# First norm of a decoder layer: loads, transposes, scaling and splitting in a new order

## The chip, the cores and the metric

The kernel runs on one core of a Trainium2 chip. The metric is device time in microseconds for one execution of the whole program; of the kernel before it is 2183.67 us, the median of three runs (2179.38 to 2184.96). The engines are named as in the profile: PE (TensorE), PEld (its weight load), DVE (VectorE), ACT (ScalarE), POOL (GpSimd), SP (SyncE, which issues most DMA transfers).

## The reference

One layer of a hybrid decoder for a prompt of 1024 tokens and 8 sequences of one new token each, D_MODEL 1024, all in float32. What the change touches is the very start, the conditioned norm `h = rmsnorm(x, w) * (1 + scale1) + shift1`:

```python
def _adaln(c, w_mod, b_mod):
    m = jax.nn.silu(c) @ w_mod + b_mod
    return jnp.split(m[:, None, :], 6, axis=-1)

sh1, sc1, gt1, sh2, sc2, gt2 = _adaln(c, lp['w_mod'], lp['b_mod'])
h = _rmsnorm(x, lp['norm1_w']) * (1 + sc1) + sh1
qkv, gdn_gate, beta_raw, a_raw, sq, sk, sv, ga, gb = _split_in(h @ lp['w_in'])
```

From `h @ w_in` come the operands of a gated delta rule (8 heads), of a sliding-window attention with sinks (16 query heads, 4 key heads), and two branch gates. Then follow the output projection, a second conditioned norm, a gated FFN of width 2816 with a causal convolution, and a last norm. Besides the two outputs y, ten states are returned.

## The kernel before

All activations stand transposed, columns of D_MODEL on the partitions: eight tiles of 128, called k = 0 to 7. The 1032 tokens (1024 and 8) are cut into three parts of 384, 384 and 264 (`PARTS`). A product in float32 is made of three in the `fp32r` format: each operand is split into a high part, rounded, and a low part, the rest, and `mm3` (lines 177 to 182) adds hi*hi, hi*lo and lo*hi. So `b1h` and `b1l`, one pair for each part, are the split h, and `wh` and `wl` a split weight of 1024 x 128.

The first norm has these pieces, all within `run`:

- `conditioning` makes silu(c), transposed, in `cT`; `vectors` loads small vectors and turns them.
- `modulation(lo)` loads a chunk of w_mod of 1024 x 512 in four transfers of 512 KB (tag `qst`, eight slots), multiplies (line 264, four products a transfer pair, 32 x 512), copies the result (line 267), turns it with `strips` (line 270) and adds the bias (line 271). Chunks 8 and 12 give scale1 of columns k = 0 to 3 and 4 to 7, chunks 0 and 4 give shift1 of the same. `norm_scale` (line 274) makes `a1` = (1 + scale1) * w.
- `norm_part` loads the tokens of a part as rows in up to three tiles (tags `raw` or `qst`), takes the sums of squares on ACT (line 291), the power -1/2 on POOL (line 125), puts the factors on diagonals, and multiplies these with ones (line 299), so that `r` holds each token's factor on all partitions (copied at line 301).
- `turn_part` turns the tiles on PE (line 190) and copies them on DVE (line 318) into four "rooms" for a part (three for the third), slots that later stages use for other things (`ROOMS`; the tags are V, kh, kl, obt, wmh, wml, raw, qst). It stores the turned x to DRAM (`xT`, line 331) for the residual.
- `modulate` does for one k: multiply the tile by a1 and r (line 341, DVE), add the shift and round (line 342, ACT), and take the rest (line 343, DVE).

In `run` the chunks go in the order 8, 0, 12, 4; the first part is loaded and turned after chunk 8, the second after chunk 12, the third after chunk 4. The first part is modulated as soon as its shifts are there, the second and third at the beginning of `attention`. Then come the first keys and queries: `project` with `w[0]` (keys) and `w[1]` (queries), part by part, each 24 products a part, into PSUM tiles `mm` of a pool with two slots. `k_out` and `q_out` copy and split the result (lines 537 to 540 and 562 to 563). Behind them come the queries of the second pair, values, and the attention groups with late modulation chunks, decays and states in between.

The order of instructions on each engine isn't written by hand here: a scheduler of the framework sorts the program by its own model of times when the kernel is built, and the engines then run these orders strictly, waiting on semaphores. `issue_after(ins)` lets an instruction stand in that order only behind `ins`.

Of the kernel before, what the change touches and what calls it, by code (L numbers as in the profile page):

```python
# [64 lines left out]
class Step:  # L65
# [118 lines left out]
    def new_parts(self):  # L184
        return [(self.t(self.b1, [P, KC, n], f"b1h{t}", F32R), self.t(self.b1, [P, KC, n], f"b1l{t}", F32R))
                for t, (_, n) in enumerate(PARTS)]

    def transpose(self, out, in_):
        p = in_.shape[0]
        self.nc.tensor.transpose(out, in_, self.ident[:p, :p])  # L190


    def vectors(self, pool, psum):
# [4 lines left out]
        nc.sync.dma_start(rows[0:48, 0, :], I["b_mod"][0].rearrange("(n p) -> n p", p=P))  # L198
        nc.sync.dma_start(rows[48:56, 0, :], I["norm1_w"][0].rearrange("(n p) -> n p", p=P))
        nc.sync.dma_start(rows[56:64, 0, :], I["norm2_w"][0].rearrange("(n p) -> n p", p=P))  # L200
        nc.sync.dma_start(rows[64:65, 0, :], I["gdn_onorm_w"])
        nc.sync.dma_start(rows[0:96, 1, :], I["gdn_conv_w"][0].rearrange("j (n p) -> (j n) p", p=P))
        rows2 = self.t(pool, [P, P], "pp")
        nc.sync.dma_start(rows2[0:66, :], I["ffn_conv_w"][0].rearrange("j (n p) -> (j n) p", p=P))
        nc.sync.dma_start(rows2[66:88, :], I["ffn_conv_b"][0].rearrange("(n p) -> n p", p=P))
# [14 lines left out]
    def conditioning(self, pool, psum):  # L220

        nc, I = self.nc, self.I
        c = self.t(pool, [9, NP], "qst", bufs=8)
        nc.sync.dma_start(c[0:8, :], I["c_sample"])
        nc.sync.dma_start(c[8:9, :], I["c_prompt"])
        th = self.t(pool, [9, NP], "qst", bufs=8)
        nc.scalar.activation(th, c, AF.Tanh, scale=0.5)
        s2 = self.t(pool, [9, NP], "qst", bufs=8)
# [22 lines left out]
    def modulation(self, pool, psum, ptag, lo, tags, rtag):  # L251
# [4 lines left out]
        for k0 in range(0, KC, 4):  # L256
# [6 lines left out]
            for j in range(4):  # L263
                nc.tensor.matmul(ps[32 * j:32 * j + 32], self.cT[:, k0 + j, :], ws[j // 2][:, j % 2, :],
                                 start=k0 == 0, stop=k0 > 0)
        rows = self.t(pool, [P, 512], rtag)
# [11 lines left out]
    def norm_part(self, pool, psum, t, tags):  # L278
# [19 lines left out]
        ps = self.t(psum, [P, 512], "pv")[:, :n]  # L298
# [5 lines left out]
    def turn_part(self, pool, psum, t, xs, tags):  # L304
# [6 lines left out]
        for c, x in enumerate(xs[:n // P]):  # L311
            k = 0
            for room in rooms:
                m = room.shape[1]
                ps = self.t(psum, [P, 4, P], "pv" if room is rooms[-1] else "pt")[:, :m]
                for i in range(m):
                    self.transpose(ps[:, i, :], x[:, (k + i) * P:(k + i + 1) * P])
                nc.vector.tensor_copy(room[:, :, c * P:(c + 1) * P], ps)
                k += m
# [9 lines left out]
        for room in rooms:  # L329
            m = room.shape[1]  # L330
            nc.sync.dma_start(self.xT[k:k + m, :, c0:c0 + n].rearrange("k p n -> p k n"), room)
# [3 lines left out]
    def modulate(self, pool, t, k, raw, r, a, sh):  # L335

        nc = self.nc
        n = PARTS[t][1] // P * P
        hi, lo = (x[:, k, :n] for x in self.h[t])
        v, s = self.t(pool, [P, 512], ("pc", "E")[k % 2])[:, :n], self.mT[:, sh + k, 8:9]  # L340
        nc.vector.scalar_tensor_tensor(v, raw, a[:, k, 8:9], r[:, :n], op0=ALU.mult, op1=ALU.mult)
        nc.scalar.activation(hi, v, AF.Identity, bias=s)
        nc.vector.scalar_tensor_tensor(lo, v, s, hi.bitcast(F32), op0=ALU.add, op1=ALU.subtract)
# [103 lines left out]
    def attention(self, pool, psum):  # L447
# [13 lines left out]
        w, raws, rs = self.start  # L461
        for t in (1, 2):
            if len(raws[t]) > KC:
                self.modulate_samples(pool, t, raws[t][KC], rs[t], self.a1, 0)
            for k in range(KC):
                self.modulate(pool, t, k, raws[t][k], rs[t], self.a1, 0)
# [1329 lines left out]
    def run(self):  # L1796
        S, nc = ExitStack, self.nc
        self.constants()
        with S() as ca:
            with S() as c:  # L1800
# [5 lines left out]
                self.h = self.new_parts()  # L1806
                self.xT = self.t(self.dr, [KC, P, NT], "xT")
                self.a1 = self.const([P, KC, 9], "a1")
                rs, raws = {}, {}
# [91 lines left out]
```

## Time and profile before

| | |
|---|---|
| median of 3 runs | 2183.67 us (2179.38 to 2184.96) |
| profiled execution, its own time | 2182.87 us |
| its span | 2181.1 us |
| PE busy | 2101.2 us, 96% |
| DVE busy | 1344.9 us, 62% |
| ACT busy | 789.0 us, 36% |
| POOL busy | 311.5 us, 14% |
| granted TensorE clock, mean | 0.972 |
| moved by DMA | 223.91 MB, mean 103 GB/s |

Times in a timeline are microseconds from the span's start. A row of a timeline has start, duration, engine, line, operation, tiles (output, then inputs), shape and count; at the end in brackets the idle time of the engine ahead of it and what released it. [...] In the groups by line, "xcount | busy, mean ns | idle before" follow the shapes.

### The profile page before, as it was taken

How to read it: one execution, taken by the hardware profiler on the slowest of the kernel's cores; microseconds unless marked ns; L12 is line 12 of the kernel's file. 1: busy time of each engine (PE TensorE's matmuls, PEld its weight loads, DVE VectorE, ACT ScalarE, POOL GpSimd, SP SyncE). 2: the span in 40 equal slices, each digit the busy share in tenths (PEclk: the TensorE clock that was granted, in tenths of full speed). 3: DMA queues.
4: the chain of work that ended last, by engine and by line, in shares of the span. 5: the costliest groups of instructions: out<-in, count | busy, mean ns of one | idle time of the engine just before them, and what ended most of it. 6: DMA issues, size and time to landing. Idle time of an engine off the chain costs nothing.

```text
span 2181.1 us, 41178 instructions
## 1 busy us (share of the span) xinstructions
PE 2101.2 (96%) x16514; PEld 1982.5 (91%) x16514; DVE 1344.9 (62%) x2907; ACT 789.0 (36%) x2010; POOL 311.5 (14%) x422
## 2 busy tenths in 40 slices
PE   7899999999899999999999999999999999999998
PEld 3886777899898998999999999999999999999998
DVE  5756676375655756765324665478876867866565
ACT  3445456333234344334322032344433433421102
POOL 1000000020321210111111200002232233100000
PEclk9999999999999989999999999999999999999999
DMA  9333323151232221221318844523222232263202
GB/s 345 113 108 114 117 74 97 48 147 47 71 84 60 71 68 40 63 65 50 91 60 237 250 152 126 155 67 98 79 88 69 78 98 68 97 224 121 85 3 79
DMA packets 265114, 223.91 MB, mean 103 GB/s; under 512 B 57586, under 2 KB 232469, under 8 KB 264906
## 3 DMA queue, kind: packets, MB, share of 16 engines
q1 hardware_dynamic: 263354, 216.83, 32.7%
q10 hardware_dynamic: 1152, 3.70, 0.4%
q8 instruction: 130, 2.13, 0.4%
q0 software_dynamic: 416, 0.75, 0.1%
q14 instruction: 62, 0.51, 0.1%
HBM read 171.25 MB, written 52.33 MB: 103 GB/s over the span
## 4 chain that ended last, share of the span: by engine, by line
PE 61%; DVE 4%; DMA 4%; ACT 2%; issue 1%; SPq 1%; POOL 1%; POOLq 0%; DVEq 0%; ACTq 0%
PE mm L180 14%; PE mm L182 13%; PE mm L181 13%; PE wv L181 3%; PE wv L180 3%; PE wv L182 3%; PE wy L182 2%; PE wy L180 2%; PE wy L181 2%; PE tp L190 1%; DMA b1l<-dlr 1%; PE rc L909 1%; PE rc L905 1%; PE rc L902 1%; DMA b2l<-ob 1%
## 5 line engine op out<-in xcount | busy, mean ns | idle before, releaser
L180 PE MATMUL mm<-b1h,wh 128*128 128x384 f32 (+1 forms) x1440 | 474.3, 331 | 8.2 <-DVE kl L540 4.3
L182 PE MATMUL mm<-b1h,wl 128*128 128x384 f32 (+1 forms) x1440 | 467.4, 326 | 0.6 <-DVE wl L130 0.5
L181 PE MATMUL mm<-b1l,wh 128*128 128x384 f32 (+1 forms) x1440 | 467.3, 325 | 0.0
L180 PEld LDWEIGHTS mm<-b1h,wh 128*128 128x128 f32 x1440 | 273.4, 190 | 17.4 <-issue 3.1
L182 PEld LDWEIGHTS mm<-b1h,wl 128*128 128x128 f32 x1440 | 272.7, 190 | 6.9 <-issue 4.4
L181 PEld LDWEIGHTS mm<-b1l,wh 128*128 128x128 f32 x1440 | 273.9, 190 | 4.5 <-issue 4.0
L130 DVE TENSOR_TENSOR wl<-raw,wh 128x1024 fp32r<-128x1024 f32 x76 | 93.5, 1230 | 81.1 <-ACT wh L129 80.2
L129 ACT ACTIVATE wh<-raw 128x1024 fp32r<-128x1024 f32 x77 | 80.6, 1047 | 168.3 <-PE mm L181 96.6
L180 PE MATMUL mm<-b2h,wh 128*128 128x384 f32 (+1 forms) x384 | 124.4, 324 | 1.8 <-ACT wh L129 1.7
L180 PE MATMUL mm<-pk,w 128*128 128x260 f32 (+1 forms) x440 | 124.7, 283 | 1.0 <-ACT pk L129 0.6
L181 PE MATMUL mm<-pk,w 128*128 128x260 f32 (+1 forms) x440 | 124.4, 283 | 0.8 <-DVE pk L130 0.8
L182 PE MATMUL mm<-b2h,wl 128*128 128x384 f32 (+1 forms) x384 | 122.9, 322 | 1.8 <-DVE wl L130 1.8
L182 PE MATMUL mm<-pk,w 128*128 128x260 f32 (+1 forms) x440 | 124.4, 283 | 0.0
L181 PE MATMUL mm<-b2l,wh 128*128 128x384 f32 (+1 forms) x384 | 123.2, 321 | 0.0
L182 PE MATMUL mm<-bmh,pk 128*128 128x256 f32 (+1 forms) x380 | 109.0, 287 | 0.9 <-DVE pk L130 0.7
L180 PE MATMUL mm<-bmh,pk 128*128 128x260 f32 (+1 forms) x380 | 108.7, 286 | 0.2 <-ACT pk L129 0.2
L1382 DVE SCALAR_TENSOR_TENSOR x<-mm,mT,x 128x256 f32<-128x256 f32 (+2 forms) x133 | 63.5, 480 | 70.6 <-PE mm L182 70.3
L181 PE MATMUL mm<-bml,pk 128*128 128x260 f32 (+1 forms) x353 | 100.8, 285 | 0.0
L180 PE MATMUL mm<-bmh,w 128*128 128x260 f32 (+1 forms) x320 | 90.9, 284 | 0.0
L182 PE MATMUL mm<-bmh,w 128*128 128x260 f32 (+1 forms) x320 | 90.8, 284 | 0.0
L130 DVE TENSOR_TENSOR w<-ws,w 128x512 fp32r<-128x512 f32 x88 | 60.2, 685 | 41.8 <-ACT w L129 41.7
L180 PEld LDWEIGHTS mm<-pk,w 128*128 128x128 f32 x440 | 82.9, 188 | 1.6 <-ACT pk L129 0.8
(595 smaller groups left out, 5701.0 us busy)
## 6 DMA issues: line engine op xcount, KB each, us to landing
raw<-in_w_in_dram SPq DMA_DIRECT2D x60, 512.0 KB
bml<-act SPq DMA_DIRECT2D x22, 516.0 KB
raw<-in_w_ffn_gate_dram SPq DMA_DIRECT2D x22, 512.0 KB
raw<-in_w_ffn_up_dram SPq DMA_DIRECT2D x22, 512.0 KB
raw<-in_w_ffn_down_dram SPq DMA_DIRECT2D x22, 512.0 KB
qst<-in_w_mod_dram SPq DMA_DIRECT2D x16, 512.0 KB
raw<-in_w_mod_dram SPq DMA_DIRECT2D x16, 512.0 KB
act<-fa SPq DMA_DIRECT2D x22, 260.0 KB
```

What stands on the lines that cost most here:

```text
L129: self.nc.scalar.activation(hi, x, AF.Copy)
L130: (eng or self.nc.vector).tensor_tensor(lo, x, hi.bitcast(F32), op=ALU.subtract)
L180: mm(ps, whi, xhi, start=first, stop=False, **kw)
L181: mm(ps, whi, xlo, start=False, stop=False, **kw)
L182: mm(ps, wlo, xhi, start=False, stop=last, **kw)
L190: self.nc.tensor.transpose(out, in_, self.ident[:p, :p])
L902: yield step(nc.tensor.matmul(ks, K[:, n, :], S, start=True, stop=True))
L905: yield step(nc.tensor.matmul(sp, W[:, n, :], y, start=True, stop=True))
L909: yield step(nc.tensor.matmul(ds, kd[:, n, :], s, start=True, stop=True))
L1382: nc.vector.scalar_tensor_tensor(x[:, :np_], ps[:, :np_], self.mT[:, m + j, 8:9], x[:, :np_], op0=ALU.mult, op1=ALU.add)
```

## The change

The loads, the turning and the splitting of the first norm get another order, and some of the work other engines.

- The chunks still go 8, 0, 12, 4, but the second part is loaded and turned after chunk 0, and the third behind chunk 4.
- Behind chunk 0 the columns 0 to 3 of the first two parts are scaled, shifted and split. Behind chunk 12 their columns 4 to 7 are scaled only; the scaled tiles stand unsplit in `vs`, which is the room of the third part's `b1h` and `b1l`, until chunk 4 gives their shifts (`shift_tile`). The third part's operands take that room behind it.
- All stores to xT wait, in SP's order, until the third part's x is issued (`store_turned`).
- Odd columns of the second and third part are scaled on ACT and multiplied by r on POOL (`scale_tile`); three of four rooms of the second part, and two of three of the third, are copied by ACT instead of DVE.
- The small loads of `vectors` are issued by ACT; `conditioning` uses the slots kh and kl.
- The projections of the first keys and queries go keys of parts one and two, queries of parts one and two, keys of part three, queries of part three, with a third PSUM slot; the keys of the first two parts stand behind the second part's last turns and the last product of chunk 4.

```diff
     def vectors(self, pool, psum):
-        nc.sync.dma_start(rows[0:48, 0, :], I["b_mod"][0].rearrange("(n p) -> n p", p=P))
+        nc.scalar.dma_start(rows[0:48, 0, :], I["b_mod"][0].rearrange("(n p) -> n p", p=P))
...
     def modulation(self, pool, psum, ptag, lo, tags, rtag):
...
+        self.chunks.append(at.ins)
...
     def turn_part(self, pool, psum, t, xs, tags):
...
+                if t == 1 and c == 2:
+                    self.turned.append(turned.ins)
+                if t and room is not rooms[0]:
+                    nc.scalar.copy(room[:, :, c * P:(c + 1) * P], ps)
+                else:
+                    nc.vector.tensor_copy(room[:, :, c * P:(c + 1) * P], ps)
...
-            nc.sync.dma_start(self.xT[k:k + m, :, c0:c0 + n].rearrange("k p n -> p k n"), room)
+            self.stores.append((self.xT[k:k + m, :, c0:c0 + n].rearrange("k p n -> p k n"), room))
...
+    def store_turned(self):
+        for dst, room in self.stores:
+            with self.tc.issue_after(self.x_load.ins):
+                stored = self.nc.sync.dma_start(dst, room)
+        self.x_load = stored
+
+    def scale_tile(self, v, t, k, raw, r):
+        nc = self.nc
+        r, a = r[:, :v.shape[1]], self.a1[:, k, 8:9]
+        if t and k % 2:
+            nc.scalar.activation(v, raw, AF.Copy, scale=a)
+            nc.gpsimd.tensor_tensor(v, v, r, op=ALU.mult)
+        else:
+            nc.vector.scalar_tensor_tensor(v, raw, a, r, op0=ALU.mult, op1=ALU.mult)
+
+    def shift_tile(self, v, t, k):
+        hi, lo = (x[:, k, :v.shape[1]] for x in self.h[t])
+        s = self.mT[:, k, 8:9]
+        self.nc.scalar.activation(hi, v, AF.Identity, bias=s)
+        self.nc.vector.scalar_tensor_tensor(lo, v, s, hi.bitcast(F32), op0=ALU.add, op1=ALU.subtract)
...
     def attention(self, pool, psum):
...
-        for t in range(3):
-            self.project(w[0], h, k_out, (t,))
-            self.project(w[1], h, q_out, (t,))
+        self.mm = [self.pmm, self.pmm, self.pmf]
+        for ts in ((0, 1), (2,)):
+            for t in ts:
+                with ExitStack() as c:
+                    for ins in self.turned + self.chunks[(3, 3)[t]:(3, 3)[t] + 1] if t < 2 else ():
+                        c.enter_context(self.tc.issue_after(ins))
+                    self.project(w[0], h, k_out, (t,))
+            self.project(w[1], h, q_out, ts)
+        self.mm = [self.pmm]
...
     def run(self):
...
+                vs = [self.t(self.b1, [P, 4, 384], f"b1{x}2") for x in "hl"]
...
                 for lo in (8, 0, 12, 4):
                     self.modulation(pool, psum, "sc", lo, (("qst", 8),), "mrows")
+                    if lo in (8, 12):
+                        self.norm_scale(self.a1, 8, self.n1w, lo - 8, lo - 4)
+                    if lo in (8, 0):
+                        part(lo == 0)
+                        w.append(self.win((COL_SQ, COL_SK)[lo == 8]))
+                    if lo == 0:
+                        for t in range(2):
+                            self.modulate(pool, t, range(4), raws[t], rs[t])
+                    for t in range(2) if lo in (12, 4) else ():
+                        for k in range(4, KC):
+                            v = vs[t][:, k - 4, :]
+                            if lo == 12:
+                                self.scale_tile(v, t, k, raws[t][k], rs[t])
+                            else:
+                                self.shift_tile(v, t, k)
+                self.h.append(self.new_part(2))
+                part(2)
+                self.store_turned()
+                self.modulate_samples(pool, 2, raws[2][KC], rs[2], self.a1, 0)
+                self.modulate(pool, 2, range(KC), raws[2], rs[2])
```

Since a scheduler sets the orders, three places show what moved. The line numbers are those of each kernel (line 264 before is line 263 of the change, 190 is 189, 331 is 344). The first is SP's queue around the last modulation chunks, before:

```order
L288 DMA qst_338<-in_x_prompt_dram 128x1024
L288 DMA qst_346<-in_x_prompt_dram 128x1024
L288 DMA qst_354<-in_x_prompt_dram 128x1024
L331 DMA xT_154<-V_210 128x4x384
L261 DMA qst_424<-in_w_mod_dram 128x2x512
L331 DMA xT_154<-kh_211 128x2x384
L331 DMA xT_154<-kl_212 128x2x384
L261 DMA qst_426<-in_w_mod_dram 128x2x512
L261 DMA qst_432<-in_w_mod_dram 128x2x512
L261 DMA qst_434<-in_w_mod_dram 128x2x512
```

and in the changed kernel (`raw_838` is the weight of the next query pair):

```order
L260 DMA qst_445<-in_w_mod_dram 128x2x512
L260 DMA qst_447<-in_w_mod_dram 128x2x512
L135 DMA raw_838<-in_w_in_dram 128x8x128
L260 DMA qst_453<-in_w_mod_dram 128x2x512
L260 DMA qst_455<-in_w_mod_dram 128x2x512
L288 DMA qst_488<-in_x_prompt_dram 128x1024
L288 DMA qst_496<-in_x_prompt_dram 128x1024
L288 DMA qst_504<-in_x_sample_dram 8x1024
L344 DMA xT_154<-V_211 128x4x384
L344 DMA xT_154<-kh_212 128x2x384
L344 DMA xT_154<-kl_213 128x2x384
```

The stores of the first part have moved from ahead of the last chunk's quarters (424 to 434 before, 445 to 455 now) to behind the third part's x. The second place is PE at the last chunk of the changed kernel. `qst_296` and `qst_304` are the second and third x tile of the second part, and `qst_455` takes the slot of `qst_304`; `mm_648` are the first keys of the first part:

```order
L270 MATMUL sc_427<-strips_119,mrows_425 128x9 x4
L189 MATMUL pt_352<-ident,qst_304 128x128 x2
L263 MATMUL sc_444<-qst_445,cTr_116 32x512 x2
L263 MATMUL sc_444<-qst_447,cTr_116 32x512 x2
L189 MATMUL pt_356<-ident,qst_304 128x128 x2
L263 MATMUL sc_444<-qst_453,cTr_116 32x512 x2
L189 MATMUL pt_360<-ident,qst_304 128x128 x2
L263 MATMUL sc_444<-qst_455,cTr_116 32x512 x2
L180 MATMUL mm_648<-b1h_10_148,wh_258 128x384
L181 MATMUL mm_648<-b1l_11_149,wh_258 128x384
L182 MATMUL mm_648<-b1h_10_148,wl_259 128x384
```

Before, PE had the keys of the first part (`mm_646`), and behind them its queries, between the products of its third chunk (`sc_312`), a whole chunk earlier:

```order
L270 MATMUL sc_290<-strips_119,mrows_288 128x9 x4
L264 MATMUL sc_312<-qst_313,cTr_116 32x512 x2
L264 MATMUL sc_312<-qst_315,cTr_116 32x512 x2
L264 MATMUL sc_312<-qst_321,cTr_116 32x512 x2
L180 MATMUL mm_646<-b1h_10_148,wh_260 128x384
L181 MATMUL mm_646<-b1l_11_149,wh_260 128x384
L182 MATMUL mm_646<-b1h_10_148,wl_261 128x384
```

So no product of keys or queries runs ahead of the last chunk any more, and the turns of the second part stand between its quarters. The third place is ACT behind the last chunk. There the changed kernel has (line 361 is the shift and rounding, 321 a copy of a room, 301 the copy of r; lines 564, 565 and 589 split keys and queries, 537, 538 and 562 before):

```order
L321 COPY qst_519<-pv_530 128x2x128
L361 ACTIVATE b1h_10_148<-b1h_14_152,mT 128x384 x4
L361 ACTIVATE b1h_12_150<-b1l_15_153,mT 128x384 x4
L321 COPY raw_518<-pt_525 128x3x128
L321 COPY qst_519<-pv_544 128x2x128
L301 COPY pp_515<-sc_513 128x264
L564 ACTIVATE kh_642<-mm_648 64x384
L565 ACTIVATE kh_642<-mm_648 64x384
L589 ACTIVATE qst_646<-mm_714 64x384
L564 ACTIVATE kh_643<-mm_648 64x384
L565 ACTIVATE kh_643<-mm_648 64x384
L564 ACTIVATE kh_642<-mm_681 64x384
```

The eight shifts of the unsplit tiles stand ahead of most of the third part's copies; its own scaling (line 352) comes two rows further on, behind the splitting of the second part's keys (`mm_681`).

More of the change, by code (lines that the diff above doesn't have):

```diff
@@ L182, in mm3, with new_part @@
         mm(ps, wlo, xhi, start=False, stop=last, **kw)
-    def new_parts(self):
-        return [(self.t(self.b1, [P, KC, n], f"b1h{t}", F32R), self.t(self.b1, [P, KC, n], f"b1l{t}", F32R))
-                for t, (_, n) in enumerate(PARTS)]
+    def new_part(self, t):
+        return tuple(self.t(self.b1, [P, KC, PARTS[t][1]], f"b1{x}{t}", F32R) for x in "hl")
     def transpose(self, out, in_):
         p = in_.shape[0]
-        self.nc.tensor.transpose(out, in_, self.ident[:p, :p])
+        return self.nc.tensor.transpose(out, in_, self.ident[:p, :p])
     def vectors(self, pool, psum):
@@ L222, in conditioning @@
         nc, I = self.nc, self.I
-        c = self.t(pool, [9, NP], "qst", bufs=8)
+        c = self.t(pool, [9, NP], "kh")
         nc.sync.dma_start(c[0:8, :], I["c_sample"])
         nc.sync.dma_start(c[8:9, :], I["c_prompt"])
-        th = self.t(pool, [9, NP], "qst", bufs=8)
+        th = self.t(pool, [9, NP], "kl")
         nc.scalar.activation(th, c, AF.Tanh, scale=0.5)
-        s2 = self.t(pool, [9, NP], "qst", bufs=8)
+        s2 = self.t(pool, [9, NP], "kh")
         nc.vector.scalar_tensor_tensor(s2, th, 1.0, c, op0=ALU.add, op1=ALU.mult)
@@ L297, in norm_part @@
             xs.append(x)
-        ps = self.t(psum, [P, 512], "pv")[:, :n]
+        ps = self.t(psum, [P, 512], "sc")[:, :n]
         nc.tensor.matmul(ps, self.ones, dg.rearrange("p c i -> p (c i)")[:, :n], start=True, stop=True)
@@ L459, in attention @@
         self.first = self.first_head(pool)
[L461 to L466, printed above, removed]
+        w = self.start
         self.delta_setup()
@@ L1805, in run, with part @@
                 self.vectors(pool, psum)
-                self.h = self.new_parts()
+                self.h = [self.new_part(t) for t in range(2)]
+                vs = [self.t(self.b1, [P, 4, 384], f"b1{x}2") for x in "hl"]
                 self.xT = self.t(self.dr, [KC, P, NT], "xT")
                 self.a1 = self.const([P, KC, 9], "a1")
-                rs, raws = {}, {}
+                rs, raws, self.stores, self.turned, self.chunks = {}, {}, [], [], []
+                w = []
+                def part(t):
+                    xs, rs[t] = self.norm_part(pool, psum, t, ["qst"] * 3 if t else ["raw", "raw", "qst"])
+                    raws[t] = self.turn_part(pool, psum, t, xs, ROOMS[t])
@@ L1810, in run @@
                 for lo in (8, 0, 12, 4):
                     self.modulation(pool, psum, "sc", lo, (("qst", 8),), "mrows")
-                    for t in {8: (0,), 12: (1,), 4: (2,)}.get(lo, ()):
-                        xs, rs[t] = self.norm_part(pool, psum, t, ["qst"] * 3 if t else ["raw", "raw", "qst"])
-                        raws[t] = self.turn_part(pool, psum, t, xs, ROOMS[t])
-                    if lo == 8:
-                        w = [self.win(COL_SK), self.win(COL_SQ)]
-                    if lo >= 8:
-                        self.norm_scale(self.a1, 8, self.n1w, lo - 8, lo - 4)
@@ L1819, in run @@
-                    for k in range(lo, lo + 4) if lo < 8 else ():
-                        self.modulate(pool, 0, k, raws[0][k], rs[0], self.a1, 0)
-                self.start = w, raws, rs
+                    if lo in (8, 12):
+                        self.norm_scale(self.a1, 8, self.n1w, lo - 8, lo - 4)
+                    if lo in (8, 0):
[4 more added lines that the diff above has]
+                            self.modulate(pool, t, range(4), raws[t], rs[t])
@@ L1822, in run @@
+                self.modulate(pool, 2, range(KC), raws[2], rs[2])
+                self.start = w
                 self.attention(pool, psum)
```

29 lines of the change are left out of this document (13 added, 16 removed).

## The prediction

> **What bounds the kernel now.** I read the page first, then the busy time by stretch of the first 100 us, then the timelines of the engines there. In the stretch rows the columns are: from and to, length, busy us and count of PE, PEld, DVE, ACT and POOL, the granted clock, DMA share, GB/s.
>
> ```profile
> span 2181.1 us, 41178 instructions
> PE 2101.2 (96%) x16514; PEld 1982.5 (91%) x16514; DVE 1344.9 (62%) x2907; ACT 789.0 (36%) x2010; POOL 311.5 (14%) x422
> ...
> 0.00:20.00 20.00, 10.40 (x49) 4.45 (x51) 8.09 (x20) 7.03 (x10) 7.81 (x33) 0.97 0.81 279
> 20.00:40.00 20.00, 17.97 (x92) 9.37 (x88) 12.21 (x30) 6.93 (x13) 1.65 (x3) 0.86 1.07 378
> 40.00:60.00 20.00, 15.53 (x76) 9.30 (x75) 14.95 (x38) 7.66 (x14) 2.62 (x3) 0.91 1.02 371
> 60.00:70.00 10.00, 5.08 (x27) 3.82 (x26) 9.83 (x22) 6.76 (x14) 0.00 (x0) 0.83 0.56 152
> 70.00:80.00 10.00, 9.94 (x49) 9.80 (x47) 8.81 (x24) 5.42 (x13) 0.53 (x1) 0.83 0.40 131
> 90.00:100.00 10.00, 10.00 (x66) 10.00 (x65) 3.44 (x5) 2.72 (x5) 0.00 (x0) 1.00 0.21 54
> ```
>
> PE is the bound of the program, but not of its start. From 20 to 60 us the DMA engines are full (share above 1, 371 to 378 GB/s). From 60 to 70 us they are not, and PE is busy for half the time while DVE is busy for 9.83 of 10 us: the tiles of the first norm are late. From about 90 us PE is full at clock 1.00, and everything behind stands in PE's order. So what the change is worth is read at one instruction: the first product with the weights of the next query pair, which both kernels issue right behind the keys and queries of the start.
>
> ```profile
> 1.54 0.32 SPq L198 DMA_DIRECT2D pc<-in_b_mod_dram  x1
> 3.66 0.35 SPq L205 DMA_DIRECT2D pp<-in_ffn_conv_b_dram  x1
> 4.05 1.94 SPq L261 DMA_DIRECT2D qst<-in_w_mod_dram  x4
> 13.45 1.06 ACT L291 ACTIVATE vch<-raw 128x1024 f32<-128x1024 f32 x1 [8.17 <-DMA raw<-in_x_prompt_dram]
> 14.79 1.06 ACT L291 ACTIVATE vch<-raw 128x1024 f32<-128x1024 f32 x1 [0.19 <-DMA raw<-in_x_prompt_dram]
> 28.08 0.38 SPq L331 DMA_DIRECT2D xT<-V  x1
> 31.99 3.99 SPq L261 DMA_DIRECT2D qst<-in_w_mod_dram  x3
> 46.15 0.44 PE L190 MATMUL pt<-ident,qst 128*128 128x128 f32 x2 [0.52 <-DVE obt L318]
> 46.52 1.05 PE L264 MATMUL sc<-qst,cTr 128*32 128x512 f32 x4
> 47.50 0.44 PE L190 MATMUL pt<-ident,qst 128*128 128x128 f32 x2
> 47.87 1.05 PE L264 MATMUL sc<-qst,cTr 128*32 128x512 f32 x4
> 86.38 0.28 PE L182 MATMUL mm<-b1h,wl 128*128 128x264 f32 x1
> 88.61 0.41 PE L180 MATMUL mm<-b1h,wh 128*128 128x384 f32 x1 [1.95 <-DVE kl L540]
> ```
>
> Line 264 at 47.87 is the product with the last quarter of the fourth modulation chunk; from it the shifts of columns 4 to 7 come. The marked product is line 180 at 88.61. The row at 86.38 is the last product of the first keys and queries. Between 47.87 and 88.61 lie 40.7 us.
>
> **The change part by part.** I make the sum for the two times, the last chunk and then the marked product.
>
> Loads at the start. The seven loads of the vectors leave SP for ACT's queue, so the first modulation load is issued at 1.54 instead of 4.05: 2.5 us earlier. Their 125 KB still move, 0.3 us at 375 KB/us (the mean of 378 and 371): 2.2 us are left. Counting back from the first x tile, which lands at 13.45 as the fifth 512 KB block, with 1.34 us a block (14.79 - 13.45), the stream starts at 6.75 before, so at 4.55 now.
>
> Bytes ahead of the last chunk. Now nothing of xT is stored before x has been issued. Ahead of and with the third quarter of the last chunk lie 15 modulation blocks, 6 x tiles and 3 weight blocks, 24 x 0.524 = 12.6 MB, and 0.4 MB of small ones: 13.0 MB, 34.7 us at 375 KB/us, so it lands at 39.2. Before, 1.6 MB of stores (V, kh, kl, from 28.08) lay in the same stream, 4.2 us.
>
> The last quarter is another matter: by the order it takes the slot of the second part's third x tile, and PE turns that tile's last piece only behind the products of the third quarter. So: 39.2, products of one quarter 0.5 (half of the 1.05 above), turn 0.4, issue 0.4, and then a block that finds an empty queue:
>
> ```profile
> oa<-sg POOLq DMA_DIRECT2D x1, 512.0 KB, 3.3
> ```
>
> That row is the only 512 KB block whose issue-to-landing time the page gives, 3.3 us. The last quarter is there at 43.8, 4.1 us before the 47.87 of now. The bounds: 40.6 if the slot comes free while the stream still runs (39.2 + 1.36), 47.9 if each further turn waits for a copy as it did at 46.15.
>
> From there to the marked product, PE's own work by rows:
>
> ```profile
> 58.08 0.52 PE L181 MATMUL mm<-b1l,wh 128*128 128x384 f32 x1
> 58.40 0.52 PE L182 MATMUL mm<-b1h,wl 128*128 128x384 f32 x1
> ...
> 75.19 0.34 PE L182 MATMUL mm<-b1h,wl 128*128 128x384 f32 x1
> 75.37 0.34 PE L180 MATMUL mm<-b1h,wh 128*128 128x384 f32 x1
> ...
> 84.69 0.28 PE L180 MATMUL mm<-b1h,wh 128*128 128x264 f32 x1
> 84.81 0.28 PE L181 MATMUL mm<-b1l,wh 128*128 128x264 f32 x1
> ```
>
> From start to start a 384-wide product costs 0.18 us at full clock and 0.32 at the low one, a 264-wide one 0.12. All 96 products of the first two parts now stand behind the last chunk, 17.0 us (at 0.177); before, 24 of them ran ahead of it. The third part's 48 cost 5.8. PE will have idled some 3 us, and after such an idle time (the rows at 58 us) some 15 products ran slow: 15 x 0.14 = 2.1. The last quarter, the strips, the row broadcast, the third part's turns and four score products: 5.5 us, by the same groups of before (0.5 + 0.9 + 0.6 + 3.0 + 0.5).
>
> What PE waits for. Beside the 1.95 at 88.61, its longest wait in those 40.7 us, and the like of it:
>
> ```profile
> 63.41 0.44 PE L190 MATMUL pv<-ident,qst 128*128 128x128 f32 x2 [1.09 <-ACT pp L301]
> 66.65 0.69 PE L190 MATMUL pv<-ident,qst 128*128 128x128 f32 x2 [2.80 <-DVE qst L318]
> ```
>
> They are turns of the third part: one waits for ACT's copy of the broadcast row, the other for a copy that stands behind other work on a full DVE. Now the other parts' scaling is done by then: behind the last chunk DVE and ACT have one operation each a tile, 0.6 us,
>
> ```profile
> L343 DVE SCALAR_TENSOR_TENSOR b1l<-E,mT,b1h 128x384 fp32r<-128x384 f32 x8 | 4.7, 606 | 0.0
> L342 ACT ACTIVATE b1h<-E,mT 128x384 fp32r<-128x384 f32 x8 | 4.7, 605 | 3.2 <-DVE E L341 3.2
> ```
>
> while PE has 12 products of columns 0 to 3 in hand for each of three projections (36 x 0.18 = 6.4 us, which is the cover; without it the 8 tiles would show, 4.8 us). A third accumulator for keys and queries takes the wait of 1.95 at 88.61 away. What is late next is the third part: its split can only be written when the unsplit tiles have left its room, and on ACT it stands behind the copies of the first keys. I leave 2.5 us of waits: 1.5 there, 0.5 for the first scores, 0.5 for the next weights.
>
> Sum: 17.0 + 5.8 + 2.1 + 5.5 + 2.5 = 32.9, so the marked product at 43.8 + 32.9 = 76.7 instead of 88.61: 11.9 us earlier.
>
> New on GpSimd are eight products of two tiles, 384 or 256 wide. Nearest rows (columns of the timeline: start, us):
>
> ```profile
> L1501 POOL TENSOR_TENSOR ws<-raw 128x512 f32<-128x512 f32 x20 | 28.2, 1410 | 46.3 <-DVE w L130 46.3
> 1529.67 1.47 POOL L1501 TENSOR_TENSOR ws<-ws,raw 128x512 f32<-128x512 f32 x1 [0.77 <-DVE w L130]
> 1530.02 1.67 DVE L1593 SCALAR_TENSOR_TENSOR fa<-fz,fcw,fa 128x512 f32<-128x512 f32 x1
> 1531.94 0.74 DVE L1593 SCALAR_TENSOR_TENSOR fa<-fz,fcw,fa 128x512 f32<-128x512 f32 x1
> ```
>
> By width 1.41 gives 1.06 and 0.71 us. Beside a running one, DVE's own took 1.67 instead of 0.74. Four of the eight lie before the last chunk, where DVE has room; the four of the third part cost nothing (they hide under the second part's queries, 4.2 us) up to 4 x (0.71 + 0.93) = 6.6 us. I take 1.5, the third part's wait above.
>
> [...]
>
> Behind the marked product PE's order is the same, buffer numbers aside, for some 530 rows. Then, in the sliding-window stage and in the later heads, the scheduler has exchanged groups; the work is equal. I take that as 0, between a gain and the losses in the third rival. The profiled execution is 2181.1 us in its span and 2182.87 in all, 0.8 under the median of 2183.67; I take the gain off the median: 2183.7 - 11.9 = 2171.8, and say 2172.
>
> **The rivals.** First, the third part becomes the bound: every GpSimd product delays DVE and its own tile in turn. For it: the DVE rows at 1530; ACT's row order. Against: PE reaches that part about 20 us behind the last chunk. Price 6.6 more: gain 5.3, 2178.
>
> Second, the change does not do what it says: the last quarter comes no earlier, since its slot hangs on turns that wait for copies. Then 47.9 + 32.9 = 80.8, gain 7.8, 2176.
>
> Third, and on the other side, the exchanged order of the window stage:
>
> ```profile
> 180.00:200.00 20.00, 17.07 (x108) 12.20 (x100) 15.13 (x53) 10.18 (x42) 0.00 (x0) 0.82 0.42 149
> 280.00:300.00 20.00, 17.02 (x102) 11.77 (x101) 12.91 (x43) 11.18 (x46) 0.00 (x0) 0.83 0.23 74
> 360.00:380.00 20.00, 15.28 (x93) 12.47 (x93) 15.24 (x43) 11.54 (x43) 0.19 (x1) 0.85 0.16 52
> ```
>
> In these three PE idles 2.9 + 3.0 + 4.7 = 10.6 us, and the clock takes another 0.5 x 20 = 10. There chains of scores, maxima and turns have no projection to fill between. If the new order leaves twice as many bare, 20.6 us go: 2192, slower. It decides from 11.9 us on; half of it makes no difference. Against: both orders have about as many bare groups.
>
> Fourth, all goes better: last quarter at 40.6, no cold products beyond 0.6, no wait for the third part: 40.6 + 29.9 = 70.5, gain 18, 2166.
>
> **How the numbers follow.** The forecast 0.52 (its own range 2167 to 2177), the better case 0.12, the third part 0.14, the chunk no earlier 0.10, the window stage 0.12. No change means within 0.3%, 6.5 us, which a measurement of this kernel can tell: 2177.1 to 2190.2. Faster: 0.52 + 0.12, 0.04 of the third part, 0.07 of the chunk: 0.75. Slower: 0.07 of the window stage. Same: 0.18. The range 2162 to 2181 reaches from a little beyond the better case to past the third part's, and leaves out the window stage's loss.
>
> **What would show it.** The fourth chunk's last product near 43.8 with an idle PE of 2 to 3 us before it; 26 products of keys and queries before the strips of that chunk; DVE no longer full from 60 to 70 us; the marked product at 74 to 79; stores of xT all behind 40 us. The forecast falls if the marked product is later than 82, if the split tiles of the third part keep PE waiting over 4 us, or if PE's idle time from 180 to 400 us has grown by more than 5 us.

## Result and profile after

The changed kernel takes 2171.31 us (median of 7 runs, 2163.95 to 2173.48), the kernel before beside it 2183.52 (7 runs, 2179.38 to 2186.22). The ratio is 0.9941, 95% interval 0.9929 to 0.9953: 12.2 us faster. The forecast was 2172. The profiled execution took 2173.48 in all, the longest of the seven, against 2182.87, so the two traces differ by 9.4 us only.

The page of the changed kernel, and its busy time by stretch (columns as before):

```profile
span 2171.8 us, 41182 instructions
PE 2086.3 (96%) x16514; PEld 1975.1 (91%) x16514; DVE 1338.0 (62%) x2886; ACT 796.4 (37%) x2031; POOL 321.5 (15%) x430
...
20.00:40.00 20.00, 15.19 (x90) 6.73 (x92) 13.39 (x30) 11.46 (x26) 3.59 (x5) 0.83 1.02 345
40.00:60.00 20.00, 19.00 (x110) 16.12 (x106) 16.99 (x35) 15.55 (x32) 5.37 (x6) 1.00 0.84 284
60.00:70.00 10.00, 5.69 (x36) 5.32 (x36) 9.69 (x23) 7.60 (x18) 3.61 (x5) 1.00 0.89 309
```

From 40 to 60 us PE is now busy for 19.00 of 20 us instead of 15.53. The picture of 60 to 70 us has hardly changed: PE busy for little over half, DVE full (9.69). Rows of the timeline of the changed kernel (lines 180 and 181 are the same as before, 263 was 264, 189 was 190, 321 and 323 are the copies of rooms on ACT and DVE, 129 and 130 are in `split`):

```profile
11.36 1.06 ACT L291 ACTIVATE vch<-raw 128x1024 f32<-128x1024 f32 x1 [5.79 <-DMA raw<-in_x_prompt_dram]
33.68 0.88 SPq L260 DMA_DIRECT2D qst<-in_w_mod_dram  x2
36.66 0.38 SPq L344 DMA_DIRECT2D xT<-V  x1
39.82 1.05 PE L263 MATMUL sc<-qst,cTr 128*32 128x512 f32 x4 [1.03 <-DMA qst<-in_w_mod_dram]
40.81 0.44 PE L189 MATMUL pt<-ident,qst 128*128 128x128 f32 x2
41.17 1.05 PE L263 MATMUL sc<-qst,cTr 128*32 128x512 f32 x4
61.37 0.66 PE L189 MATMUL pt<-ident,qst 8*128 8x8 f32 x8 [1.96 <-ACT raw L321]
69.37 0.51 PE L180 MATMUL mm<-b1h,wh 128*128 128x264 f32 x2 [2.82 <-ACT b1h L129]
70.80 0.59 PE L181 MATMUL mm<-b1l,wh 128*128 128x264 f32 x1 [0.92 <-DVE b1l L130]
78.00 0.34 PE L180 MATMUL mm<-b1h,wh 128*128 128x384 f32 x1
1152.34 0.28 PE L1125 MATMUL sm<-ones,b1l 128*128 128x1 f32 x2
```

The last quarter of the fourth chunk is multiplied at 41.17 (47.87 before), the marked product comes at 78.00 (88.61 before): 10.6 us earlier. Between them lie 36.8 us (40.7 before); PE's longer waits there are now three, all for the third part, 5.7 us together. The last row is the first product into a tile `sm`, at the start of the branches, behind the window stage and all eight heads. It stood at 1164.87 before, so there 12.5 us are in hand; in this execution 3.2 of them are lost again behind it.

### The profile page after: what moved, and what is told of

The parts are those of the page before. It is cut to its first block, busy times and chain, and to the rows that moved or that the text cites. A ratio compares the mean times of both kernels' runs of the same rounds, so it can differ in the third digit from the quotient of the medians.

```text
span 2171.8 us, 41182 instructions
## 1 busy us (share of the span) xinstructions
PE 2086.3 (96%) x16514; PEld 1975.1 (91%) x16514; DVE 1338.0 (62%) x2886; ACT 796.4 (37%) x2031; POOL 321.5 (15%) x430
## 4 chain that ended last, share of the span: by engine, by line
PE 59%; DVE 5%; DMA 4%; ACT 2%; issue 2%; SPq 1%; POOL 1%; POOLq 0%; DVEq 0%; ACTq 0%
PE mm L180 13%; PE mm L182 13%; PE mm L181 13%; PE wv L181 3%; PE wv L180 3%; PE wv L182 3%; PE wy L182 2%; PE wy L180 2%; PE wy L181 2%; DMA b1l<-dlr 1%; PE tp L189 1%; ACT osq L870 1%; DMA b2l<-ob 1%; DVE wl L130 1%; SPq L1103 1%
```

## The experiments

Four columns of the table come from each kernel's profiled execution, in us: the end of the fourth chunk's last product (start and duration of its row), the marked product, the first product into `sm`, and the time between these two. The ratios are those against the kernel before, with their intervals.

| kernel | chunk over | marked product | first `sm` | marked to `sm` | median | ratio (interval) |
|---|---|---|---|---|---|---|
| before | 48.92 | 88.61 | 1164.87 | 1076.3 | 2183.52 | |
| changed | 42.22 | 78.00 | 1152.34 | 1074.3 | 2171.31 | 0.9941 (0.9929 to 0.9953) |
| vectors_on_sp | 44.29 | 80.97 | 1156.80 | 1075.8 | 2173.63 | 0.9958 (0.9941 to 0.9974) |
| stores_early | 48.55 | 85.42 | 1160.08 | 1074.7 | 2178.08 | 0.9983 (0.9974 to 0.9992) |
| loads_alone | 45.12 | 87.28 | 1161.89 | 1074.6 | 2185.59 | 1.0013 (1.0002 to 1.0025) |
| work_alone | 50.22 | 86.91 | 1168.49 | 1081.6 | 2185.01 | 1.0019 (1.0006 to 1.0031) |
| copies_on_dve | 43.84 | 79.43 | 1163.02 | 1083.6 | 2182.73 | 1.0009 (1.0000 to 1.0018) |
| scaling_on_dve | 43.13 | 79.95 | 1156.41 | 1076.5 | 2171.18 | 0.9942 (0.9924 to 0.9961) |
| two_slots | 43.25 | 79.26 | 1152.48 | 1073.2 | 2170.59 | 0.9947 (0.9932 to 0.9962) |
| products_ahead | 43.76 | 82.09 | 1154.49 | 1072.4 | 2171.68 | 0.9955 (0.9940 to 0.9970) |
| late_states | 42.66 | 79.27 | 1150.54 | 1071.3 | 2167.60 | 0.9932 (0.9906 to 0.9957) |
| samples_first | 43.60 | 74.30 | 1160.51 | 1086.2 | 2174.13 | 0.9963 (0.9949 to 0.9977) |
| samples_late | 42.09 | 72.53 | 1148.32 | 1075.8 | 2168.76 | 0.9940 (0.9926 to 0.9954) |
| samples_mods | 42.54 | 74.04 | 1150.42 | 1076.4 | 2167.29 | 0.9939 (0.9925 to 0.9952) |

How far such a mark can be trusted: late_states has the changed kernel's PE order well past the marked product and comes 1.3 us later there; samples_first, samples_late and samples_mods share a start, too, and lie within 1.8 us. So a difference under some 1.8 us at the marked product shows nothing by itself. On the way from there to `sm` two pairs of kernels have nearly the same order on PE: in the built programs two_slots and late_states differ in 12 of the 6608 products between the two marks, scaling_on_dve and products_ahead in 140. Their ways differ by 1.9 and 4.1 us, so there a difference under some 4 us shows nothing.

### The loads: vectors_on_sp and stores_early

```diff
-        nc.scalar.dma_start(rows[0:48, 0, :], I["b_mod"][0].rearrange("(n p) -> n p", p=P))
+        nc.sync.dma_start(rows[0:48, 0, :], I["b_mod"][0].rearrange("(n p) -> n p", p=P))
...
```

> The changed kernel, but the seven small loads of the vectors go back from ACT's queue to SP. By the prediction's first step the stream of the large loads starts 2.2 to 2.5 us later and the fourth chunk's last quarter product goes from 41.17 to about 43.5; nothing behind it changes, so the marked product goes from 78.00 to about 80.3, and of the 10.6 us gained there 8.3 are left. Rival, that the stretch behind the chunk is bound by the third part and not by the chunk: the chunk is later, but the marked product stays within 0.7 us of 78.00.

The timeline of vectors_on_sp:

```profile
13.07 1.06 ACT L291 ACTIVATE vch<-raw 128x1024 f32<-128x1024 f32 x1 [7.80 <-DMA raw<-in_x_prompt_dram]
43.23 1.06 PE L263 MATMUL sc<-qst,cTr 128*32 128x512 f32 x8
```

The first x tile is there 1.7 us later (13.07 against 11.36), the chunk is over 2.1 later, the marked product comes 3.0 later. The term of the start (2.2 us) is borne out within that scatter, and the stretch behind the chunk does not absorb it.

```diff
-            self.stores.append((self.xT[k:k + m, :, c0:c0 + n].rearrange("k p n -> p k n"), room))
+            nc.sync.dma_start(self.xT[k:k + m, :, c0:c0 + n].rearrange("k p n -> p k n"), room)
...
-                self.store_turned()
```

> The changed kernel, but each part's stores to xT are issued right behind its turns again. In SP's order four of them (kl, V, kh, wml: 1.97 MB) then stand ahead of the chunk's last quarter. By bytes alone (375 KB/us) it comes 5.2 us later: product at 46.4 instead of 41.17, marked product at about 83.2 instead of 78.00, half of the gain given back. Rival, that stores cost more than their bytes because SP waits in order for the copy of the room that a store reads, with the loads behind it: last quarter later than 48.5. Second rival, that the end of the stream was not the limit: less than 2 us later.

The timeline of stores_early:

```profile
40.97 1.05 PE L263 MATMUL sc<-qst,cTr 128*32 128x512 f32 x4
45.14 3.41 PE L263 MATMUL sc<-qst,cTr 128*32 128x512 f32 x16 [1.00 <-DVE mT L271]
```

The fourth chunk's sixteen products run in one piece from 45.14, released by the strips of the third chunk (`mT`), whose own last products stand at 40.97; the chunk is over at 48.55, 6.3 us later than in the changed kernel, the marked product 7.4 later. The row holds the four quarters as two pairs, and the last pair starts at 46.85: 0.4 later than by bytes alone (46.4), and ahead of the 48.5 that SP's waits would need. But PE does not wait for a transfer here; the lateness has come in by the third chunk, whose last products stood at 33.95 in the changed kernel. Part of the 6.3 is not the stores': the granted clock is 0.50 from 45 to 48 us, so the four quarters take 3.4 us, about twice what they take at full clock (in the changed kernel a pair took 1.0 us at 37.36). Of the gain of 0.59% there is 0.17% left.

### Loads and work, each alone

loads_alone is the kernel before with these loads (vectors by ACT, `kh` and `kl` for the conditioning, late stores); work_alone is the changed kernel with the loads of before, that is, with both edits above and

```diff
-        c = self.t(pool, [9, NP], "kh")
+        c = self.t(pool, [9, NP], "qst", bufs=8)
...
```

> The kernel before with the loads of the change alone: vectors by ACT, the conditioning in the slots kh and kl, all stores to xT behind the third part's x. Scaling, turns, engines, order of parts and projections stay. By the prediction's first two steps the fourth chunk's last quarter comes 2.2 us (start of the stream) and 4.2 us (1.6 MB of stores) earlier, at about 41.5 instead of 47.87, and if that chunk sets the marked product it comes at about 82.2 instead of 88.61. Rival: from 60 to 70 us DVE is full with the scaling, splitting and copies of the second and third part, all behind the chunk; then the chunk's 6 us are eaten by DVE and the marked product comes at 86 or later.

The timeline of loads_alone, and its row from 60 to 70 us:

```profile
44.07 1.05 PE L264 MATMUL sc<-qst,cTr 128*32 128x512 f32 x4
60.84 0.55 PE L190 MATMUL pt<-ident,qst 128*128 128x128 f32 x3 [1.71 <-DVE raw L318]
66.73 1.01 PE L190 MATMUL pt<-ident,qst 8*128 8x8 f32 x8 [1.09 <-DVE raw L318]
87.28 0.41 PE L180 MATMUL mm<-b1h,wh 128*128 128x384 f32 x1 [1.95 <-DVE kl L547]
```

```profile
60.00:70.00 10.00, 6.24 (x27) 4.80 (x28) 9.75 (x21) 4.63 (x10) 0.00 (x0) 0.65 0.30 107
```

The chunk comes 3.8 us earlier, not the 6.4 expected, and 2.5 of these are eaten behind it: DVE is full (9.75 of 10 us), and PE's turns of the third part wait for its copies. That is the rival's case; at the end there is no gain.

> The changed kernel with the loads of before (vectors on SP, conditioning in qst slots, stores right behind the turns), but with the new order of scaling, the unsplit tiles, the work on ACT and GpSimd and the new order of parts: the counterpart of loads_alone, which gained 1.3 us at the marked product. If loads and work are two terms that add, as the prediction has it, the work alone brings what is left of the 10.6: marked product at about 79.3. If each only counts with the other (an earlier chunk meets a full DVE; a free DVE waits for a late chunk), both alone bring little: marked product at 86 to 89. Between them, by the runs vectors_on_sp (2.97 lost) and stores_early (7.42 lost) added up: 88.4.

The last products of the chunk in work_alone:

```profile
46.98 3.24 PE L263 MATMUL sc<-qst,cTr 128*32 128x512 f32 x8 [1.78 <-DMA qst<-in_w_mod_dram]
```

Here PE waits for the chunk (1.78 for a transfer); it is over at 50.22, and the stretch behind it is 36.7 us instead of the 39.7 of before. The granted clock is 0.50 from 47 to 50 us, so some of this chunk's lateness is the clock's. The marked product gains 1.7, the end nothing. So loads alone bring 1.3 us at the marked product, work alone 1.7, and both together 10.6: some 7.6 us exist only where both are done. The 1.3 and the 1.7 are no more than such a mark can scatter (1.8 above); the 7.6 is far more. With the old work, DVE is what is late once the chunk comes early; with the old loads, the chunk is what a freed DVE waits for.

### The third part: scaling_on_dve, copies_on_dve, samples_first

```diff
-        if t and k % 2:
+        if False:
             nc.scalar.activation(v, raw, AF.Copy, scale=a)
             nc.gpsimd.tensor_tensor(v, v, r, op=ALU.mult)
```

> The changed kernel with all scaling on DVE as before: eight ACT operations and eight GpSimd products (1.32 and 0.73 us each) less, eight DVE operations (0.61 and 0.47 us) more, four of them in the third part. The prediction's first rival (each GpSimd product delays DVE and its own tile) expects the marked product up to 5 us earlier, 73 to 76; the forecast, that they are hidden, 77 to 79; a DVE that is full to the end gives it 4 x 0.47 = 1.9 us later, about 80.

The marked product comes at 79.95, 1.95 us later than with GpSimd, not up to 5 us earlier, as the rival had it. That speaks for a full DVE and against a GpSimd that is in the way. (The chunk is 0.9 later in this execution, so half of the 1.95 may be that. PE's wait for the samples, 2.82 in the changed kernel, is 3.62.) In the median nothing is left of it. What GpSimd cost can be seen in the changed kernel, in its groups and on DVE beside it:

```profile
L353 POOL TENSOR_TENSOR E<-E,pp 128x384 f32<-128x384 f32 x2 | 2.6, 1320 | 9.2 <-ACT E L352 9.2
62.66 1.62 POOL L353 TENSOR_TENSOR E<-E,pp 128x256 f32<-128x256 f32 x2 [0.98 <-ACT E L352]
62.67 1.01 DVE L362 SCALAR_TENSOR_TENSOR b1l<-pc,mT,b1h 128x256 fp32r<-128x256 f32 x1
65.02 0.47 DVE L362 SCALAR_TENSOR_TENSOR b1l<-E,mT,b1h 128x256 fp32r<-128x256 f32 x1
```

A 384-wide product takes 1.32 us (the estimate was 1.06). Beside a 256-wide one DVE's operation took 1.01 us instead of 0.47. The 384-wide ones, ahead of the strips, cost DVE too: its scaling of a tile took 1.36 us beside one (at 42.81) and 0.61 without (at 44.63). What makes DVE's operations longer beside them was not shown. But by the marked product taking the products off GpSimd gained nothing: what DVE is spared weighs at least as much.

```diff
-                if t and room is not rooms[0]:
+                if False:
                     nc.scalar.copy(room[:, :, c * P:(c + 1) * P], ps)
```

> The changed kernel with all room copies on DVE again (17 copies of 0.37 to 0.48 us each leave ACT). If DVE's load is what held the stretch behind the chunk before, the second part's copies make the last turns late and the third part's copies stand in DVE behind the keys: chunk or marked product 3 to 6 us later (81 to 84). Rival: the copies on ACT stand behind the keys' and queries' copies there (the 1.96 us at the samples' turn), and going back costs nothing: marked product 77 to 79.5.

At the marked product the rival holds: 79.43, 1.4 us later, with the chunk 1.6 later. PE's waits of the third part have turned into one of 3.97 for the split keys behind DVE's copies:

```profile
67.12 0.69 PE L180 MATMUL mm<-b1h,wh 128*128 128x384 f32 x1 [3.97 <-DVE kl L567]
```

But the whole gain is gone at the end (ratio 1.0009), and it goes behind the start: from the marked product to `sm` it takes 1083.6 us instead of 1074.3. Neither expectation had that.

```diff
+        if n < PARTS[t][1]:
+            ps = self.t(psum, [P, KC, NS], "pt")
+            for k in range(KC):
+                self.transpose(ps[:, k, :], xs[-1][:NS, k * P:(k + 1) * P])
...
         for c, x in enumerate(xs[:n // P]):
...
-        if n < PARTS[t][1]:
-            ps = self.t(psum, [P, KC, NS], "pt")
...
```

> The changed kernel, but in the third part the eight columns of the samples are turned and copied ahead of the prompt's tiles, not behind them. Theory: the 5.7 us that PE waits between 58 and 71 us (1.96 at the samples' turn, 2.82 and 0.92 at the first product of the third part), and about 1.7 us of low clock behind them, are the samples' chain of seven small operations, which stands last in a full DVE queue; with the chain ahead, the marked product comes at 72.5 to 75 instead of 78.00, and the median at about 2167. Rival, that DVE as a whole is the bound there (busy 9.69 of 10 us): the wait passes to the last split tile of the third part, and the marked product gains less than 1.5 us.

In the changed kernel the samples' chain on DVE (lines 330 to 378 and 130) runs from 63.71 to 70.52, one operation at a time between the other tiles':

```profile
63.71 0.23 DVE L330 COPY o<-pt 128x64 f32<-128x64 f32 x1
64.89 0.21 DVE L376 TENSOR_TENSOR o<-o,pp 128x64 f32<-128x64 f32 x1
67.09 0.23 DVE L377 TENSOR_TENSOR o<-o,a 128x64 f32<-128x64 f32 x1
68.81 0.22 DVE L378 TENSOR_TENSOR o<-o,mT 128x64 f32<-128x64 f32 x1
70.52 0.23 DVE L130 TENSOR_TENSOR b1l<-o,b1h 128x64 fp32r<-128x64 f32 x1
```

In samples_first the first product of the third part and the marked product are

```profile
68.63 0.39 PE L180 MATMUL mm<-b1h,wh 128*128 128x264 f32 x1 [0.47 <-DVE kl L567]
74.30 0.45 PE L180 MATMUL mm<-b1h,wh 128*128 128x384 f32 x1 [0.78 <-ACT wh L129]
```

From the chunk's end to the marked product there are 30.7 us instead of 35.8: the theory is right, those 5 us are the samples' chain (its waits and the low clock behind them). They are saved although DVE has as much to do as before. Yet at the end this kernel is no faster than the changed one (2174.13). It loses 12 us on the way to `sm`.

### Behind the start: late_states, samples_late, samples_mods

In copies_on_dve and samples_first, two kernels with different starts, PE's order is the same, buffer numbers aside, from the marked product on until far behind `sm`. They take 1083.6 and 1086.2 us for that way, against 1071 to 1077 in all others but work_alone (1081.6, with another order). This points to the order. The test is to keep a start and change the order behind it:

```diff
-                self.later(lambda: self.conv_states(pool, psum), 100)
+                self.later(lambda: self.conv_states(pool, psum), 300)
```

That is late_states on the changed kernel and samples_late on samples_first; samples_mods changes the 100 of `self.later(lambda: next(self.mods), 100)` to 0.

> The changed kernel with one priority changed far behind the start: the convolution states' turns get a priority offset of 300 instead of 100, so that PE's order is word for word the same for some 740 rows (to about 260 us) and then exchanges groups. The prediction took the exchanged order at nothing, between a gain and losses. If that holds, the median is within 1.5 us of the changed kernel's. If the order of groups is worth as much as the traces of the first runs suggest (5 us won or lost behind an equal start), the marked product stays at 78.0 and the first U of the next stage, at 459.99 in the changed kernel, comes 3 to 8 us later, of which part stays in the median.

The marked product is 1.3 us later (79.27), `sm` 1.8 earlier (1150.54), the median 2167.60, from four runs between 2162.01 and 2173.31. This is neither case of the expectation, and by the intervals the kernel is not told apart from the changed one. The first write of `U`, with which the heads begin, comes at 465.94, 6.0 us later, but `sm` is not late, so this mark alone decides nothing.

> samples_first with the priority of late_states: PE's order is that of samples_first for the first 770 rows (marked product at 74 to 75), another behind it. samples_first stood 3.7 us ahead of the changed kernel at the marked product and no better at the end. If that loss lies in the order that the scheduler drew for the window stage, another draw gives the 3.7 us or part of them: median 2164 to 2168. If it is a price of the early start itself (weights of the next pair late, waits of 0.78 and 0.64 us), the median stays at 2171 or above.

> samples_first with another single priority changed (late modulation chunks offset by 0 instead of 100): the same start, PE's order another one from row 854 on. A second draw of the same question: 2164 to 2168 if the loss of samples_first was in its order behind the start, 2171 or more if it is the price of the start.

The way from the marked product to `sm` is 1075.8 and 1076.4 us, 10 less than with the same start in samples_first, and the medians are 2168.76 (just outside the expected 2164 to 2168) and 2167.29 instead of 2174.13. So most of the loss was the order's, not the early start's. The medians show 5 to 7 us of the 10: the profiled execution of samples_first was the longest of its six (2178.85).

Where the time goes can be seen on PE. Its busy time and the clock on the way up to 470 us, for the changed kernel, copies_on_dve and samples_first in turn:

```profile
78.00:470.00 392.00, 377.48 (x2411) 318.08 (x2410) 238.56 (x617) 182.56 (x612) 28.02 (x58) 0.97 0.33 102
79.43:470.00 390.57, 373.91 (x2330) 309.35 (x2329) 230.19 (x605) 181.89 (x609) 24.46 (x49) 0.96 0.31 98
74.30:470.00 395.70, 378.26 (x2357) 312.90 (x2358) 233.26 (x609) 183.87 (x612) 26.36 (x52) 0.96 0.31 100
```

and from 470 us to `sm`, for the changed kernel, samples_first and samples_late:

```profile
470.00:1152.34 682.34, 655.45 (x5779) 630.33 (x5778) 379.96 (x839) 252.80 (x734) 123.17 (x178) 0.97 0.27 72
470.00:1160.51 690.51, 663.43 (x5832) 640.55 (x5831) 384.17 (x846) 251.54 (x737) 122.05 (x183) 0.97 0.27 72
470.00:1148.32 678.32, 658.77 (x5814) 634.86 (x5814) 383.13 (x844) 253.68 (x735) 121.62 (x183) 0.97 0.27 74
```

Against the changed kernel the two lose ahead of 470 us, in the window stage: PE idles 16.7 and 17.4 us instead of 14.5, and by the trace's clock record the clock is at 0.50 for 34.1 us in both instead of 20.5, which costs up to 6.8 more. Their first `U` comes 9.8 and 11.1 us later, counted from the marked product; from 470 us on the three idle alike (26.9, 27.0 and 27.1). samples_late gains elsewhere: it idles 19.6 us behind 470. So no single place or wait is the cause. One wait that names line 1049 as releaser, DVE's transposes for the inverses of the heads, is long in both slow kernels (us in total, times, longest; 2.1 in the changed kernel), but nearly as long in late_states, whose way is the shortest:

```profile
PE tp L1052 <- DVE MR L1049: 7.4, 5, 1.8
PE tp L1052 <- DVE MR L1049: 6.4, 4, 1.8
```

What makes one order better than another was not worked out.

Whether samples_first with a better order beats the changed kernel is not settled: its ratios 0.9940 and 0.9939 lie on 0.9941, though it stands 2 to 4 us ahead at `sm`.

### The order of the products: two_slots and products_ahead

```diff
-        self.mm = [self.pmm, self.pmm, self.pmf]
         for ts in ((0, 1), (2,)):
```

> The changed kernel, but the first keys and queries have the two PSUM slots of before, not three. By the prediction the wait of 1.95 us for the split of the keys comes back, and nothing else: marked product at about 80 instead of 78.00. Rival, that with two slots the queries of a part cannot run beside its keys, so that PE has fewer products of columns 0 to 3 to hide the last chunk's shift and split behind: a bare wait of 3 to 5 us at the strips of that chunk (about 47 to 52 us), marked product at 82 or later.

The wait is back, nearly as it was (1.73), and one of 2.57 has come in at 61.13. But the marked product loses only 1.3 us, since PE no longer waits for the samples' split in this order; the strips do not stand bare, as the rival had it, and the end loses nothing. Two rows of two_slots:

```profile
61.13 0.69 PE L180 MATMUL mm<-b1h,wh 128*128 128x384 f32 x1 [2.57 <-DVE kl L566]
79.26 0.41 PE L180 MATMUL mm<-b1h,wh 128*128 128x384 f32 x1 [1.73 <-DVE kl L566]
```

```diff
-                    for ins in self.turned + self.chunks[(3, 3)[t]:(3, 3)[t] + 1] if t < 2 else ():
-                        c.enter_context(self.tc.issue_after(ins))
```

> The changed kernel without the rule that the keys of parts one and two stand behind the last turns and the last chunk: 24 products of columns 0 to 3 (4.2 us at full clock) then run in PE's idle time ahead of the chunks. Theory that PE's own work behind the chunk counts: marked product 3 to 4 us earlier, about 74.5. Theory that the third part's samples chain sets the end (ready at 70.5 whatever PE did): the products ahead only lengthen the wait, marked product 77 to 78.5. Rival: the products delay the turns and the chunk's products, the chunk is later than 42.5 and the marked product later than 79.

The third case holds, and the loss is larger than its chunk's: the chunk is over 1.5 us later, the marked product comes 4.1 later. The timeline of products_ahead:

```profile
45.42 0.44 PE L189 MATMUL pt<-ident,qst 128*128 128x128 f32 x2 [1.66 <-DVE obt L323]
72.03 0.81 PE L180 MATMUL mm<-b1h,wh 128*128 128x264 f32 x2 [3.92 <-ACT b1h L129]
82.09 0.34 PE L180 MATMUL mm<-b1h,wh 128*128 128x384 f32 x1
```

PE did 24 products early and then waited 3.92 us for the samples instead of 2.82. The median (2171.68) does not tell it from the changed kernel; the order behind differs here too (1072.4).

## Why the prediction was right, and where it was not

The time, 2172 against 2171.31, and the marked product, 76.7 against 78.00, were hit; the terms below them less well. The marked product was hit in part by luck: the last quarter came 2.6 us earlier than forecast, the stretch behind it took 3.9 longer, and these two errors leave 1.3.

- **The start of the stream**: 2.2 us forecast, 2.1 measured by the first x tile (13.45 to 11.36); in vectors_on_sp 1.7 by that tile and 2.1 by the chunk.
- **The last quarter**: 43.8 forecast, 41.17 measured. The step that failed is that its slot hangs on the last turn of the second part's third tile. Its transfer was issued in the pair at 33.68, seven us ahead of that turn (40.81), so it did not wait for it. In the built program `qst_455` has the address of `qst_411`, a quarter of the third chunk, and not that of `qst_304`. PE found the data there at 41.17, without a wait. The third quarter was used at 39.82, against 39.2 forecast: the stream was right, the lower bound (40.6) was nearly the case, and the second rival fell with it. Instead of 2 to 3 us PE idled 1.03, and ahead of the third quarter.
- **The stretch behind it**: 32.9 forecast, 36.8 measured. The term of 1.5 us for the third part was mis-sized: it kept PE waiting 5.7. The other two waits of the forecast, 0.5 each, did not come. The condition set for this (split tiles keep PE waiting over 4 us) was missed by little, 2.82 + 0.92, and the turn's 1.96 comes on top. The mechanism was one that the prediction did not name: not GpSimd, as in the first rival, which scaling_on_dve speaks against, but the eight samples: their small operations, five of them on DVE, stand between and behind the others in a full DVE's queue, while every product of the part needs them. The low clock, 2.1 us forecast behind the chunk, came behind the waits at 69.37 and 70.80 (granted clock 0.50 from 70.8 to 74.2) and took 1.5: the 14 products from 70.80 to 74.04 need 1.7 us at full clock (0.12 from start to start, as behind 74.23), not 3.2. (The rows at 58 us, from which the forecast took 15 slow products, show nine.) By subtraction 6.8 us are left for the rest, 5.5 in the forecast.
- **DVE from 60 to 70 us**: no longer full, said the prediction; it is (9.69). The splitting of the keys and the third part have moved into the time where the second part's scaling was. Full or not did not decide; the place of the samples in it did.
- **The sum**: it follows one path, the chunk and then the stretch behind it. For the whole change this path held (41.17 + 36.8). But the two terms cannot be read as gains of two parts of the change, 4.1 and 7.8 us: loads_alone and work_alone bring 1.3 and 1.7 of 10.6. The marked product follows the later of two chains, the chunk's transfers and DVE's work, and the change shortened both.
- **Behind the marked product, 0**: in the changed kernel 2.0 us were won on the way to `sm` and 3.2 lost behind it, which is near enough to 0 (a difference under 4 us on that way shows nothing). As a step it was luck. The third rival's mechanism, another order behind the start, is as large as the change itself: 10 us in copies_on_dve and samples_first, lost against the changed kernel in the window stage, where the prediction looked for it. The order that the changed kernel was given happened to be one without this loss, so the hit does not show that the chance of 0.12 was right.
- **The small signs**: 27 products of keys and queries ahead of the strips (26 forecast); PE's idle time from 180 to 400 us fell by about 1 us; the stores of xT begin at 36.66, not behind 40, since the last x was issued earlier.

## What to carry to other kernels

Two chains that end in the same place do not add: before a gain on one is counted, work out where the other then stands, and test each part of a change alone. Where a scheduler orders the program, a change at the start also draws a new order for all that follows; compare kernels at a mark right behind the change as well as at the end, and try a second order before a good or a bad end is put down to the change. Look in a full engine's queue for the operation that stands last and that everything needs, however small.

## What was not expected of the hardware

The clock's fall did not always come with the wait. In the changed kernel the 264-wide products behind the wait at 70.80 are slow at once (0.22 us from start to start, in rows of 0.42), and at full clock (0.12, in rows of 0.28) from 74.2 on:

```profile
73.60 0.42 PE L181 MATMUL mm<-b1l,wh 128*128 128x264 f32 x1
73.82 0.42 PE L182 MATMUL mm<-b1h,wl 128*128 128x264 f32 x1
...
74.35 0.28 PE L182 MATMUL mm<-b1h,wl 128*128 128x264 f32 x1
```

In late_states, with the same order, they begin at 0.12 and slow down to 0.21 only at 73.15, in the middle of an unbroken stream:

```profile
72.07 0.39 PE L181 MATMUL mm<-b1l,wh 128*128 128x264 f32 x1 [0.92 <-DVE b1l L130]
72.30 0.28 PE L182 MATMUL mm<-b1h,wl 128*128 128x264 f32 x1
72.42 0.28 PE L180 MATMUL mm<-b1h,wh 128*128 128x264 f32 x1
...
73.15 0.42 PE L180 MATMUL mm<-b1h,wh 128*128 128x264 f32 x1
73.36 0.42 PE L181 MATMUL mm<-b1l,wh 128*128 128x264 f32 x1
```

In the changed kernel the granted clock is 0.50 from 70.8 to 74.2; in late_states the slow rows reach from 73.1 to 76.5: 3.4 us each, at different places of the same stream. What sets the place was not shown.
